# Where the residual scale is applied: to the summed products in the layer norm instead of to weight rows on GpSimd

## Chip, cores and metric

One NeuronCore of one Trainium2 chip runs the kernel. The metric is device time in microseconds, the median of several runs; a single profiled execution gives the trace.

## What is computed

The reference is a decoder trunk of two layers over 256 tokens of width 1024. Each layer has two blocks, a mixer (three kinds of attention side by side) and a channel mixer (dense SwiGLU in layer 0, top-2 of 8 experts in layer 1), and each block ends in the same way:

```python
y = hybrid_mixer(h, w_in[l], ..., w_out[l], ...)        # ends in concat(ya, yb, yc) @ w_out
x = layer_norm(DEEPNORM_ALPHA * x + (1.0 + g1) * y, ln1_g[l], ln1_b[l])
...
y = swiglu(h, w1_dense[l // 2], w3_dense[l // 2], w2_dense[l // 2])   # layer 0; ends in ... @ w2
x = layer_norm(DEEPNORM_ALPHA * x + (1.0 + g2) * y, ln2_g[l], ln2_b[l])
```

The gate (1 + g) is one row of 1024 values per layer and block, computed from the conditioning vector. Since y ends in a product with w_out or w2, the row may be multiplied into the columns of these weights or into the finished sum. The kernel holds x without the factor alpha, so its row is (1 + g) / alpha, called `grow`.

## The kernel before

All activations and weights are float32. A product is made exact enough by splitting both operands into a rounded high part and the rest, hi and lo, and adding three matmuls: hi by hi, hi by lo, lo by hi. Tokens are in two row blocks of 128 (b = 0, 1).

Weights are streamed in one fixed order (`stream`). `load_ahead` issues their loads from the SP queue into `raw` tiles of 1 MB as these come free; `split_up_to` walks the same stream, ACT writes the high half (`whi`, L374) and DVE the low half (`wlo`, L377), and a raw tile is free when both of its parts are split. The order of the instructions on each engine is that of the program (the schedule is written out by hand), so an engine that waits holds up all that stands behind it.

The stages of the span are the mixer of layer 0 (up to about 190 us), the dense block (190 to 410 us), the mixer of layer 1 (410 to 566 us) and the experts (to 1440 us). In the dense block a turn t makes 256 columns of the hidden layer (`up`, L1135 to L1137), then adds the product of the previous 256 with two row blocks of w2 (`down`, L1190) into four PSUM banks, `acc[b][hf]`, one for each row block b and column half hf. In the turns DVE also sums rows of w_ada (L527, L529) for layer 1.

`gained` (L301) multiplies raw rows of w_out and w2 by `grow` on GpSimd (POOL), two instructions of 128x1024 for each raw tile, in place, before ACT and DVE split them. Three w_out tiles of layer 0, eleven w2 tiles and four w_out tiles of layer 1 go that way, 36 instructions. The first tile of w_out in layer 0 is scaled on DVE instead (L373), between its load and its split, in two instructions of 128x1024.

`layer_norm` (L705 to L717) closes a block: for each column half it adds the PSUM bank to `xres` (L711) and takes statistics (L712), then it aggregates, POOL computes the reciprocal root (L437, L438), and DVE writes `xhat` (L717), which PE turns (L638) for the next block. The last products of a block are issued row block by row block, and within one both column halves alternate:

```python
for b in range(NB):
    for k in (3, 2, 1, 0):
        out(k, ws[k], b)
    ...
    layer_norm(acc[b], xhat, b)
    if b == 0:
        split_up_to(used[0] + 4) if l == 0 else load_ahead()
```

POOL also does the affine part of the residual (`residual`, L725 and L726, eight instructions of 128x512 for each layer norm but the last), and small sums.

## Time and profile before

| | us |
|---|---|
| median of 3 runs | 1461.44 |
| lowest, highest | 1459.02, 1462.02 |
| the profiled execution's own time | 1462.73 |
| its span in the trace | 1460.9 |

The span is what the trace covers, from the first to the last instruction; the execution's own time is 1.83 us longer, and all comparisons are made against it. A stretch of the span is named by its start and end in us from the start of the span. "Granted clock" is the share of full speed that the chip gave TensorE.

### The profile page before, as it was taken

The numbers are of one execution on the slowest core, as the hardware profiler recorded it, in microseconds if no ns is written. First come the engines' busy times: TensorE is split into PE (matmuls) and PEld (weight loads), VectorE is DVE, ScalarE is ACT, GpSimd is POOL, SyncE is SP. The second block draws the span as 40 slices with busy tenths as digits, with TensorE's granted clock in tenths as the row PEclk, the third lists the DMA queues.
The fourth block names the chain that finished last, engine by engine and source line by source line (L and its number), as shares of the span: only waits on it lengthen the run. The fifth ranks groups of instructions, "written<-read, shape, count | busy, mean of one in ns | idle before, by whom it ended". The sixth has DMA issues, their size and how long they took to land.

```text
span 1460.9 us, 20619 instructions
## 1 busy us (share of the span) xinstructions
PE 1387.4 (95%) x8017; PEld 729.5 (50%) x8017; DVE 597.4 (41%) x1063; ACT 375.7 (26%) x705; POOL 191.4 (13%) x146
## 2 busy tenths in 40 slices
PE   6999899899998899999999999999999999999994
PEld 5777689899878677223233223343233342232331
DVE  3658688999877985211120121110320110320113
ACT  2464354333345542212101112011211110211100
POOL 0202344333334420000300000000000000000000
PEclk9999899999999999999999999999999999999998
DMA  8894587688656328998999999999999999999994
GB/s 319 280 339 169 199 305 256 213 266 284 233 169 208 115 97 334 408 377 324 389 403 408 408 403 408 408 402 409 409 402 409 409 402 408 409 400 408 407 402 155
DMA packets 175497, 480.47 MB, mean 329 GB/s; under 512 B 10848, under 2 KB 44184, under 8 KB 175392
## 3 DMA queue, kind: packets, MB, share of 16 engines
q1 hardware_dynamic: 173820, 475.03, 85.7%
q10 hardware_dynamic: 1572, 4.04, 0.8%
q8 instruction: 65, 1.06, 0.3%
q14 instruction: 40, 0.33, 0.1%
HBM read 477.99 MB, written 1.05 MB: 328 GB/s over the span
## 4 chain that ended last, share of the span: by engine, by line
PE 71%; DVE 16%; issue 6%; DMA 4%; ACT 2%; POOL 1%; SPq 0%; DVEq 0%; ACTq 0%; POOLq 0%
PE bk L1570 26%; PE bk L1624 12%; PE bk L1578 7%; DVE wlo L377 7%; PE bk L1630 4%; PE bk L1085 3%; PE bk L1409 2%; PE bk L1649 2%; DVE part L529 2%; PE bk L1190 2%; DMA rawwlo<-in_w_moe 2%; PE bk L1609 1%; PE bk L561 1%; ACT whi L374 1%; DMA raw<-in_w_moe 1%
## 5 line engine op out<-in xcount | busy, mean ns | idle before, releaser
L1570 PE MATMUL bk<-raw,xe 128*64 128x512 f32 x1072 | 286.2, 597 | 3.2 <-DMA raw<-in_w_moe 3.2
L377 DVE TENSOR_TENSOR wlo<-raw,whi 128x1024 fp32r<-128x1024 f32 (+3 forms) x146 | 198.3, 1394 | 38.7 <-ACT whi L374 38.6
L1590 DVE TENSOR_TENSOR eg<-aff,bk 64x512 f32<-64x512 f32 x56 | 38.0, 679 | 387.2 <-ACT aff L1589 385.4
L1570 PEld LDWEIGHTS bk<-raw,xe 128*64 128x64 f32 x1072 | 84.0, 136 | 130.2 <-issue 118.0
L374 ACT ACTIVATE whi<-raw 128x1024 fp32r<-128x1024 f32 (+3 forms) x146 | 134.6, 975 | 15.4 <-DVE raw L373 6.0
L1624 PE MATMUL bk<-raw,egT 128*64 128x512 f32 x568 | 134.4, 600 | 0.0
L301 POOL TENSOR_TENSOR raw<-raw,grow 128x1024 f32<-128x1024 f32 x36 | 97.9, 2745 | 139.8 <-DMA raw<-in_w_dense 76.6
L1570 PE MATMUL bk<-rawwhi,xe 128*64 128x512 f32 x360 | 109.5, 601 | 2.3 <-DMA rawwhi<-in_w_moe 2.3
L1570 PE MATMUL bk<-rawwlo,xe 128*64 128x512 f32 x360 | 107.3, 592 | 0.0
L685 POOL TENSOR_TENSOR part<-vrows,cf 78x512 f32<-78x512 f32 x8 | 8.5, 1062 | 743.6 <-DVE eg L1600 714.2
L1589 ACT ACTIVATE aff<-bk 64x512 f32<-64x512 f32 x56 | 33.2, 594 | 267.1 <-PE bk L1570 267.1
L1614 DVE COPY egT<-bk 128x384 f32<-128x384 f32 (+1 forms) x24 | 11.8, 491 | 214.8 <-PE bk L1609 214.8
L1137 PE MATMUL bk<-hT,wlo 128*128 128x256 f32 x320 | 92.2, 288 | 5.1 <-DVE wlo L377 5.1
L1612 ACT ACTIVATE egT<-bk 128x384 f32<-128x384 f32 (+1 forms) x32 | 14.0, 438 | 321.6 <-PE bk L1609 321.6
L1135 PE MATMUL bk<-hT,whi 128*128 128x256 f32 x320 | 92.2, 288 | 0.9 <-ACT whi L374 0.9
L1136 PE MATMUL bk<-hT,whi 128*128 128x256 f32 x320 | 91.7, 287 | 0.0
L740 PE MATMUL bk<-whi,hT 128*128 128x384 f32 (+2 forms) x208 | 78.9, 379 | 4.8 <-ACT hT L1258 2.4
L1624 PEld LDWEIGHTS bk<-raw,egT 128*64 128x64 f32 x568 | 36.7, 136 | 78.6 <-issue 65.3
L741 PE MATMUL bk<-wlo,hT 128*128 128x384 f32 (+2 forms) x208 | 74.0, 356 | 1.9 <-DVE wlo L377 1.9
L1578 PE MATMUL bk<-raw,xe 128*32 128x512 f32 x536 | 75.0, 598 | 0.0
L742 PE MATMUL bk<-whi,hT 128*128 128x384 f32 (+2 forms) x208 | 73.8, 355 | 0.1
L1137 PEld LDWEIGHTS bk<-hT,wlo 128*128 128x128 f32 x320 | 62.5, 195 | 6.2 <-DVE wlo L377 6.2
(324 smaller groups left out, 2120.2 us busy)
## 6 DMA issues: line engine op xcount, KB each, us to landing
raw<-in_w_moe SPq DMA_DIRECT2D x205, 1024.0 KB, 14.5
rawwhi<-in_w_moe SPq DMA_DIRECT2D x131, 512.0 KB, 11.5
rawwlo<-in_w_moe SPq DMA_DIRECT2D x131, 512.0 KB, 11.4
raw<-in_w_ada SPq DMA_DIRECT2D x48, 1024.0 KB, 5.2
raw<-in_w_dense SPq DMA_DIRECT2D x33, 1024.0 KB, 9.0
raw<-in_w_in SPq DMA_DIRECT2D x16, 768.0 KB, 9.1
raw<-in_w_in SPq DMA_DIRECT2D x8, 1024.0 KB, 7.8
raw<-in_w_out SPq DMA_DIRECT2D x8, 1024.0 KB, 5.2
```

The costliest lines, as they stand in the source:

```text
L301: pool.tensor_mul(raw["sb"][:, k], raw["sb"][:, k], grow[raw["gain"]])
L374: act.activation(hi, src, AF.Copy)
L377: eng.tensor_sub(lo, src, hi.bitcast(FT))
L740: mm(pss[b][:, :w], hT[0][:, k, sl], wh[:, i % 2], start=k == 0, stop=False)
L741: mm(pss[b][:, :w], hT[0][:, k, sl], wl[:, i % 2], start=False, stop=False)
L742: mm(pss[b][:, :w], hT[1][:, k, sl], wh[:, i % 2], start=False, stop=k == KD - 1)
L1135: mm(o, w[0][:, k], hT[0][:, k], start=k == 0, stop=False)
L1136: mm(o, w[0][:, k], hT[1][:, k], start=False, stop=False)
L1137: mm(o, w[1][:, k], hT[0][:, k], start=False, stop=k == KD - 1)
L1570: mm(h[hf][q:q + 64], xe[:, k, 0:BASE], at(w, i)[:, sl], start=k == 0, stop=k == KD - 1)
L1578: mm(hov[hf][q:q + 32], xe[:, k, BASE:CAP], at(w, i)[:, sl], start=k < 2, stop=k >= KD - 2)
L1624: mm(y[64 * hf:64 * hf + 64], gT[:, j, 0:BASE], at(w, i)[:, 512 * hf:512 * hf + 512], start=c == 0 and j == 0, stop=c == 3 and j == n - 1)
```

## The change

`gained`, its calls, the flags `gain` and `late` and the DVE multiplication L373 go. `layer_norm` gets the row as `gain` and multiplies each PSUM bank by its half of the row, in place, before the addition. The last products of a block (two w_out tiles, two w2 tiles) are issued by column halves: for a row block first all products of half 0, then all of half 1. The fourth block end, behind the experts, is not touched.

```diff
--- before.py
+++ after.py
@@ -114,7 +114,6 @@
 MIX_POOL = (0, 0)
 DENSE_POOL = 0
 SUMS_AHEAD = 3
-GAIN_AHEAD = 3
 BIAS_ON_DVE = 1
 GATHER_AT = 2
 ROWS_AT = (0, 2)
@@ -150,11 +149,8 @@
 
     grow = {}
 
-    def weight(key, ap, cols=False, gain=None, late=False):
+    def weight(key, ap, cols=False):
         raw = {"ap": ap.rearrange("(k p) f -> p k f", p=128), "cols": cols}
-        if gain is not None:
-            raw["gain"] = gain
-            raw["late"] = late
         for i in (1, 0) if key[0] == "out" else (0, 1):
             unit(key, raw, i)
 
@@ -233,7 +229,7 @@
         for g in OUT_ORDER:
             if g == LAST_ADA:
                 one_ada()
-            weight(("out", l, g), a["w_out"][l][256 * g:256 * g + 256], gain=(l, 0), late=l == 0 and g > 2)
+            weight(("out", l, g), a["w_out"][l][256 * g:256 * g + 256])
         if l == 0:
             ada_weights(0, 11, 12)
             for t in range(12):
@@ -241,7 +237,7 @@
                     pair_weights([(i, (f"d{i}", t), a[f"w{i}_dense"][0][:, 256 * t:256 * t + 256])
                                   for i in (1, 3)], t > 0)
                 for d in () if t in (0, 10) else (t - 1,) if t < 11 else (9, 10):
-                    weight(("d2", d), a["w2_dense"][0][256 * d:256 * d + 256], gain=(0, 1))
+                    weight(("d2", d), a["w2_dense"][0][256 * d:256 * d + 256])
                 if t in DENSE_ADA:
                     n = DENSE_ADA[t]
                     ada_weights(1, n, n + 1)
@@ -293,12 +289,6 @@
             order_of_raws.append(raw)
         elif part == 1 and all(raw is not r for r in order_of_raws[-3:]):
             order_of_raws.append(raw)
-
-    def gained(raw):
-        if "gain" in raw and not raw["late"] and "gained" not in raw and raw["gain"] in grow:
-            raw["gained"] = True
-            for k in range(2):
-                pool.tensor_mul(raw["sb"][:, k], raw["sb"][:, k], grow[raw["gain"]])
 
     def load_ahead(most=1000):
 
@@ -346,8 +336,6 @@
         for raw in order_of_raws[loads[1]:loads[1] + SUMS_AHEAD]:
             if "ada" in raw and "sb" in raw and raw["ada"][:2] not in on_pe:
                 summed(raw)
-        for raw in order_of_raws[loads[1]:min(loads[0], loads[1] + GAIN_AHEAD)]:
-            gained(raw)
         while len(ready) <= min(n, len(stream) - 1):
             raw, part = stream[len(ready)]
             key = keys[len(ready)]
@@ -358,7 +346,6 @@
             load_ahead()
             if "sb" not in raw:
                 return
-            gained(raw)
             k, f = raw["ap"].shape[1], raw["ap"].shape[2]
             if raw["cols"]:
                 f //= 2
@@ -366,11 +353,8 @@
             else:
                 k //= 2
                 src = raw["sb"][:, k * part:k * part + k]
-            assert "gain" not in raw or raw["late"] or "gained" in raw
             hi = wsplit.tile([128, 1024], FR, name="whi", tag="whi")[:, :k * f].rearrange("p (k f) -> p k f", k=k)
             lo = wsplit.tile([128, 1024], FR, name="wlo", tag="wlo")[:, :k * f].rearrange("p (k f) -> p k f", k=k)
-            if "gain" in raw and raw["late"]:
-                vec.tensor_mul(src, src, grow[raw["gain"]][:, None, :])
             act.activation(hi, src, AF.Copy)
             many = DENSE_POOL if key[0][0] == "d" and len(key) == 3 else MIX_POOL[key[1]]
             eng = pool if many and len(ready) % many == 1 else vec
@@ -702,12 +686,14 @@
         return base.tile([128, NB, D], FT, name="xhat", tag=tag)
 
 
-    def layer_norm(y, dst, b):
+    def layer_norm(y, dst, b, gain=None):
 
         st = small.tile([128, 2, 6], FT, name="lnst")
         for h in range(2):
             sl = slice(512 * h, 512 * h + 512)
             if y is not None:
+                if gain is not None:
+                    vec.tensor_mul(y[h], y[h], gain[:, sl])
                 vec.tensor_add(xres[:, b, sl], y[h], xres[:, b, sl])
             vec.bn_stats(st[:, h], xres[:, b, sl])
         mv = small.tile([128, 2], FT, name="lnmv")
@@ -1078,10 +1064,10 @@
             tick(START_TICK[l])
             acc = [[bank() for _ in range(2)] for _ in range(NB)]
 
-            def out(k, w, b):
+            def out(k, w, b, hfs=range(2)):
                 sl = slice(128 * b, 128 * b + 128)
                 for x, wi, first in ((yT[0], 0, True), (yT[0], 1, False), (yT[1], 0, False)):
-                    for hf in range(2):
+                    for hf in hfs:
                         mm(acc[b][hf], x[:, k, sl], w[wi][:, 0, 512 * hf:512 * hf + 512],
                            start=k == 7 and first, stop=k == 0 and x is yT[1])
 
@@ -1103,11 +1089,12 @@
         split_up_to(used[0] + END_SPLIT[l])
         xhat = normal(xtag)
         for b in range(NB):
-            for k in (3, 2, 1, 0):
-                out(k, ws[k], b)
+            for hf in range(2):
+                for k in (3, 2, 1, 0):
+                    out(k, ws[k], b, (hf,))
             if b == 1 and hook is not None:
                 hook(xhat, mod)
-            layer_norm(acc[b], xhat, b)
+            layer_norm(acc[b], xhat, b, grow[l, 0])
             if b == 0:
                 split_up_to(used[0] + 4) if l == 0 else load_ahead()
         return xhat, mod
@@ -1183,10 +1170,10 @@
                     gs.append((hi, lo))
                 return gs
 
-            def part(b, t, j, g, w):
+            def part(b, t, j, g, w, hfs=range(2)):
                 sl = slice(128 * b, 128 * b + 128)
                 for gi, wi in ((0, 0), (0, 1), (1, 0)):
-                    for hf in range(2):
+                    for hf in hfs:
                         mm(acc[b][hf], g[gi][:, sl], w[wi][:, 0, 512 * hf:512 * hf + 512],
                            start=t == 0 and j == 0 and gi == 0 and wi == 0, stop=t == 10 and j == 1 and gi == 1)
 
@@ -1213,11 +1200,12 @@
             ends = [(t, j, need("d2", t, j, ahead=0)) for t in (9, 10) for j in range(2)]
             split_up_to(used[0] + END_SPLIT[2])
             for b in range(NB):
-                for t, j, w in ends:
-                    part(b, t, j, gs[t][j], w)
+                for hf in range(2):
+                    for t, j, w in ends:
+                        part(b, t, j, gs[t][j], w, (hf,))
                 if b == 1:
                     hook(xhat, mod)
-                layer_norm(acc[b], xhat, b)
+                layer_norm(acc[b], xhat, b, grow[0, 1])
                 if b == 0:
                     split_up_to(used[0] + 4)
         return xhat, mod
```

On POOL, from the rope additions of the layer 0 mixer to the end of the dense block, before (L666 rope, L301 the row scaling, L437 and L438 the reciprocal root, L650 a low half, L725 and L726 the residual):

```order
L301 TENSOR_TENSOR raw<-raw,grow 128x1024 x4
L725 TENSOR_TENSOR xres<-xhat,lnrow 128x512
L726 TENSOR_TENSOR xres<-xres,lnrow 128x512
L301 TENSOR_TENSOR raw<-raw,grow 128x1024 x2
L725 TENSOR_TENSOR xres<-xhat,lnrow 128x512
L726 TENSOR_TENSOR xres<-xres,lnrow 128x512
L301 TENSOR_TENSOR raw<-raw,grow 128x1024 x2
L725 TENSOR_TENSOR xres<-xhat,lnrow 128x512
L726 TENSOR_TENSOR xres<-xres,lnrow 128x512
```

Now, the same place (L711 and L712 are the former L725 and L726):

```order
L711 TENSOR_TENSOR xres<-xhat,lnrow 128x512
L712 TENSOR_TENSOR xres<-xres,lnrow 128x512
L711 TENSOR_TENSOR xres<-xhat,lnrow 128x512
L712 TENSOR_TENSOR xres<-xres,lnrow 128x512
L711 TENSOR_TENSOR xres<-xhat,lnrow 128x512
L712 TENSOR_TENSOR xres<-xres,lnrow 128x512
L711 TENSOR_TENSOR xres<-xhat,lnrow 128x512
L712 TENSOR_TENSOR xres<-xres,lnrow 128x512
L421 TENSOR_SCALAR lnrs<-lnmv 128x1
```

The residual's eight instructions now stand in one row, without the twenty-two scalings of w2 that stood before, between and behind them.

On DVE, in the mixer of layer 0 before the retention steps, before (L854 a low half of the attention's output, L1064 the copy of a projection):

```order
L854 TENSOR_TENSOR yT_447<-bk,yT_446 128x256
L373 TENSOR_TENSOR raw<-raw,grow 128x1024
L377 TENSOR_TENSOR wlo<-raw,whi 128x1024
L854 TENSOR_TENSOR yT_447<-bk,yT_446 128x256
L373 TENSOR_TENSOR raw<-raw,grow 128x1024
L377 TENSOR_TENSOR wlo<-raw,whi 128x1024
L1064 COPY rvg<-bk 128x512 x2
```

Now:

```order
L840 TENSOR_TENSOR yT_447<-bk,yT_446 128x256
L361 TENSOR_TENSOR wlo<-raw,whi 128x1024
L840 TENSOR_TENSOR yT_447<-bk,yT_446 128x256
L361 TENSOR_TENSOR wlo<-raw,whi 128x1024
L1050 COPY rvg<-bk 128x512 x2
```

The two scalings are gone from between the splits; the other rows stand in the same order.

On PE, the last products of the dense block, row block 0, before (bk_1902 is column half 0, bk_1903 column half 1; whi and wlo are w2, ghi and glo the hidden layer):

```order
L1190 MATMUL bk_1902<-whi_3821,ghi_3645 128x512
L1190 MATMUL bk_1903<-whi_3821,ghi_3645 128x512
L1190 MATMUL bk_1902<-wlo_3822,ghi_3645 128x512
L1190 MATMUL bk_1903<-wlo_3822,ghi_3645 128x512
L1190 MATMUL bk_1902<-whi_3821,glo_3646 128x512
L1190 MATMUL bk_1903<-whi_3821,glo_3646 128x512
```

Now (bk_1898 is half 0, bk_1899 half 1), the last three of half 0 and the first three of half 1:

```order
L1177 MATMUL bk_1898<-whi_3872,ghi_3857 128x512
L1177 MATMUL bk_1898<-wlo_3873,ghi_3857 128x512
L1177 MATMUL bk_1898<-whi_3872,glo_3858 128x512
L1177 MATMUL bk_1899<-whi_3797,ghi_3623 128x512
L1177 MATMUL bk_1899<-wlo_3798,ghi_3623 128x512
L1177 MATMUL bk_1899<-whi_3797,glo_3624 128x512
```

Twelve products of half 0 come first and twelve of half 1 behind them, where they alternated.

## Rows read from the trace of the kernel before

**Rows 1.** the page: busy time of the engines, share of the span, instructions

```profile
PE 1387.4 (95%) x8017; PEld 729.5 (50%) x8017; DVE 597.4 (41%) x1063; ACT 375.7 (26%) x705; POOL 191.4 (13%) x146
```

**Rows 2.** stretches: busy us (instructions) by engine, granted clock, DMA share, GB/s

```profile
130.00:165.00 35.00, 30.67 (x172) 23.52 (x171) 28.35 (x68) 10.92 (x19) 17.69 (x12) 0.85 0.45 163
190.00:230.00 40.00, 37.34 (x280) 33.91 (x273) 33.77 (x34) 23.51 (x39) 22.95 (x11) 1.00 0.90 317
230.00:300.00 70.00, 65.73 (x459) 61.10 (x458) 63.86 (x62) 23.08 (x35) 29.63 (x13) 0.98 0.74 250
300.00:380.00 80.00, 77.56 (x535) 72.70 (x534) 72.09 (x80) 32.70 (x45) 20.60 (x8) 0.96 0.81 280
380.00:397.00 17.00, 13.93 (x106) 12.15 (x104) 15.78 (x15) 2.97 (x5) 8.40 (x3) 0.90 0.34 113
476.00:540.00 64.00, 57.30 (x306) 45.16 (x305) 58.97 (x149) 31.36 (x70) 25.59 (x14) 0.92 0.29 100
548.00:1440.00 892.00, 882.37 (x4837) 300.71 (x4837) 159.72 (x311) 134.44 (x262) 20.09 (x20) 1.00 1.01 396
```

**Rows 3.** PE's waits, 130 to 540 us: releaser, us, times, longest

```profile
PE bk L1137 <- DVE wlo L377: 5.1, 4, 3.1
...
PE bk L1014 <- DVE rst L1003: 3.8, 2, 2.0
PE bk L1190 <- DVE wlo L377: 3.8, 1, 3.8
PE bk L850 <- ACT pT L839: 3.0, 2, 2.0
PE bk L998 <- DVE rvg L1064: 2.4, 1, 2.4
```

**Rows 4.** line L301 on POOL: duration in ns, min/median/max

```profile
L301 POOL TENSOR_TENSOR raw<-raw,grow x36: 2352/2538/3388, 134.0 to 519.4; 128x1024 f32<-128x1024 f32 x36
```

**Rows 5.** DVE's groups, 190 to 400 us: shapes, count | busy us, mean ns

```profile
L377 DVE TENSOR_TENSOR wlo<-raw,whi 128x1024 fp32r<-128x1024 f32 x63 | 105.4, 1713 | 6.1 <-ACT whi L374 6.1
L529 DVE SCALAR_TENSOR_TENSOR part<-raw,cs,part 128x512 f32<-128x512 f32 x56 | 50.1, 894 | 1.7
L1144 DVE TENSOR_TENSOR glo<-g,ghi 128x256 fp32r<-128x256 f32 x20 | 14.3, 715 | 9.7 <-ACT ghi L1143 9.7
L1140 DVE TENSOR_TENSOR g<-g,bk 128x256 f32<-128x256 f32 x20 | 8.2, 410 | 0.9 <-ACT g L1139 0.9
```

**Rows 6.** DVE in one turn of the dense loop: start us, us, instruction

```profile
330.70 4.56 DVE L377 TENSOR_TENSOR wlo<-raw,whi 128x1024 fp32r<-128x1024 f32 x2
...
339.57 3.50 DVE L377 TENSOR_TENSOR wlo<-raw,whi 128x1024 fp32r<-128x1024 f32 x3 [0.53 <-ACT whi L374]
...
349.97 1.22 DVE L377 TENSOR_TENSOR wlo<-raw,whi 128x1024 fp32r<-128x1024 f32 x1
```

**Rows 7.** POOL in the same turn

```profile
331.78 5.75 POOL L301 TENSOR_TENSOR raw<-raw,grow 128x1024 f32<-128x1024 f32 x2 [13.52 <-DMA raw<-in_w_dense]
```

**Rows 8.** DVE in the mixer of layer 1, softmax steps

```profile
482.81 1.79 DVE L805 TENSOR_SCALAR smm<-smm 128x2 f32<-128x2 f32 x1
...
490.73 0.17 DVE L805 TENSOR_SCALAR smm<-smm 128x2 f32<-128x2 f32 x1
```

**Rows 9.** DVE in the mixer of layer 0, rows of w_out scaled on DVE

```profile
141.50 1.21 DVE L373 TENSOR_TENSOR raw<-raw,grow 128x1024 f32<-128x1024 f32 x1
143.84 1.23 DVE L377 TENSOR_TENSOR wlo<-raw,whi 128x1024 fp32r<-128x1024 f32 x1 [1.12 <-ACT whi L374]
```

**Rows 10.** DVE at the end of the dense block, around the layer norm

```profile
403.45 0.69 DVE L711 TENSOR_TENSOR xres<-bk,xres 128x512 f32<-128x512 f32 x1 [0.29 <-PE bk L1190]
...
409.85 0.68 DVE L711 TENSOR_TENSOR xres<-bk,xres 128x512 f32<-128x512 f32 x1
```

**Rows 11.** line L1085 on PE: weight loads and matmuls, ns

```profile
L1085 PEld LDWEIGHTS bk<-whi,yT x128: 186/188/333, 158.0 to 561.0; 128*128 128x128 f32 x128
L1085 PE MATMUL bk<-whi,yT x128: 387/394/774, 158.1 to 561.3; 128*128 128x512 f32 x128
```

## The prediction, before the run

> **What bounds the kernel now.** I began with the page's engine totals: PE is busy 95% of the span, DVE 41%, POOL 13% [rows 1]. A share over the whole span hides that the stages differ, so the next view is the table of stretches [rows 2]. From 548 to 1440 us, the experts, PE is busy 882.37 of 892 us and the DMA engines are full (share 1.01). The change touches nothing there. That stage begins when the mixer of layer 1 ends and frees its memory, and then runs at its own pace, so a microsecond won before it moves the end by a microsecond. What counts is how much time PE loses before 548 us, and to whom.
>
> I count PE's loss in a stretch as idle time plus what a lowered clock costs, (1 - granted clock) x busy time. From [rows 2]:
> - 130 to 165 (mixer 0): 4.33 + 0.15 x 30.67 = 8.9 us
> - 190 to 230 (start of the dense block): 2.7 us
> - 230 to 300, 300 to 380, 380 to 397 (dense turns): 5.6 + 5.5 + 4.5 = 15.6 us
> - 476 to 540 (mixer 1): 6.70 + 0.08 x 57.30 = 11.3 us
>
> Together 38.5 us. PE's waits say to whom [rows 3]: in the dense block to DVE's low halves (L1137 and L1190, 8.9 us), in the mixers to DVE's rst and rvg (3.8 and 2.4 us) and to ACT's pT, which itself comes late behind DVE's softmax steps. DVE is full there: 63.86 of 70 us, 72.09 of 80, 58.97 of 64 [rows 2].
>
> Part of DVE's fullness is not work. POOL's scaling L301 takes 2.35 to 3.39 us for each of 36 instructions [rows 4]. While it runs, DVE instructions that read SBUF alone are stretched. Two low halves take 4.56 us at 330.70, where three take 3.50 at 339.57, 1.17 each [rows 6]; POOL is in L301 from 331.78 to 337.5 [rows 7]. In mixer 1 a tiny L805 takes 1.79 us beside L301 and 0.17 without [rows 8]. An instruction that reads a PSUM bank is not stretched: L1140 averages 0.41 us over the same stage [rows 5]. From 190 to 400 us the 63 low halves average 1.713 us [rows 5], so on them alone DVE loses 63 x (1.713 - 1.17) = 34 us. A few of these are due to the residual's own POOL work, which stays.
>
> **The change part by part.**
>
> *Dense block, 22 L301 removed.* The turn from 330.70 to 349.97 lasts 19.27 us [rows 6]. DVE is busy 72.09/80 of it, 17.4 us, and 2 x (2.28 - 1.17) = 2.2 us of that is the stretch of two low halves; L1144, 0.715 us on average [rows 5], gives back something over half a microsecond more. DVE then needs under 15 us and the short waits for ACT. PE needs 19.27 minus its loss, 5.5 us over 4.15 turns, or 17.9 us. So PE becomes the bound of the turn, with about 2 us to spare on DVE. Of the 15.6 us I take back 14; the rest stays as short waits. In 190 to 230 I take nothing of the 2.7 us: there the residual's eight POOL instructions move up into the place of L301, as the order on POOL shows, and stretch DVE in its stead. Bounds: 8 us (half of the loss has other causes) and 18.3 us (all of both).
>
> *Mixer 0, six L301 and two L373 removed.* Each L373 holds DVE 1.21 us, and then DVE waits 1.12 us until ACT has made the high half of the scaled rows [rows 9]. That is 4.7 us off DVE just ahead of rvg, on which PE waits 2.4 us, and of rst, on which it waits about 2 [rows 3]. The two L301 before them stretched softmax steps as well. I expect the first wait to go, half of the second, and about half of the slow clock that follows (4.6 us in the stretch): 2.4 + 1 + 2.3, say 6 us. Bounds: 0 (PE's chain of scores, rst and products is the slow part) and 8.9.
>
> *Mixer 1, eight L301 removed.* Eight stretches of about 1.6 us [rows 8] are some 13 us of DVE time, more than the 11.3 us that PE loses. The softmax chain also has round trips between PE, ACT and DVE that no scaling causes, so I take 8 us. Bounds: 4 and 11.3.
>
> *Layer norm, 12 multiplications added.* The nearest row is L711, which reads a bank and a row of SBUF: 0.69 us [rows 10]; 12 x 0.69 = 8.3 us of DVE. For row block 0 the three steps of half 0 now run beside the products of half 1, and three steps instead of four follow the last product: 0.7 us earlier. For row block 1 DVE comes late: L711 starts at 409.85, straight behind the two splits [rows 10], when its products are done, so all six steps follow, 1.4 us more and 0.7 net. PE turns that block right then. At the ends of mixer 0 and the dense block that is +0.7 us each; at the end of mixer 1 no splits stand between, and I put 0. Sum +1.4; bounds -2.1 (0.7 earlier at all three) and +8.3 (all twelve on the path).
>
> *Column halves on PE.* Two matmuls in a row used one stationary tile before, and now each follows another. The trace has a weight load of 186 to 188 ns for each matmul, 128 for 128, whether the tile is the same or not [rows 11]; nothing was shared, so I cost this at nothing. The Trainium skill says otherwise of the plan (TensorE: Matmul & The Clock Gate, Step-by-step: what each phase is for): loading is separate from multiplying so that one load can serve several matmuls. By it, the new order would give up one load of each pair.
>
> *The rest.* The order on SP and ACT is the same, and no DMA is added; a w2 tile no longer waits for POOL between landing and split. The row `grow` must now live until the layer norm, so ACT's write of the next row may wait for the last multiplication; it stands behind other ACT work, and uncovered it would cost one step, 0.7 us.
>
> Sum: -14 - 6 - 8 + 1.4 = -26.6 us. The profiled execution took 1462.73 us, which gives 1436.1; its time lies 1.29 us over the median, so against the median I predict **1435 us**.
>
> **The rivals.**
>
> *Half the gain (the next wait is close behind).* The five loads of a turn are 5.24 MB; at share 0.81 the DMA engines moved 280 GB/s [rows 2], so full engines move 346 GB/s and need 15.2 us of the 17.9 that PE needs. That fits, but the loads come in bursts as tiles come free. In the mixers the round trips may hold PE as DVE did. Half of 28 us is left, less 1.4: 1449 us. Chance 0.22.
>
> *The whole loss comes back.* 8.9 + 15.6 + 11.3 - 1.4 = 34.4 us: 1427 us. For it speaks that a low clock follows PE's own pauses. Chance 0.12.
>
> *Slower: the stretch has another cause and stays.* If DVE were slow in these places by something else, such as the DMA writes of the same stretches, PE's loss would remain and the multiplications would come on top, 1.4 to 8.3 us: 1463 to 1470, about 1465 us. It decides if a 128x1024 low half still takes over 2 us where POOL is idle. Against it stand 3.50 us for three while DMA runs, and 0.17 against 1.79 [rows 6, 8]. Chance 0.03.
>
> *The weight loads were shared.* Three block ends have 144 such matmuls; if the second of each of 72 pairs paid another 0.19 us [rows 11], that is 13.7 us: 1449 us. Chance 0.03.
>
> *It does not do what it says.* The order shows the L301 rows gone, so only the halves can fail: if DVE were let go only after both halves, every row block would have six steps behind its products, 1.4 us each at six places instead of +1.4 in all, 1442 us. I count that within the first case.
>
> **How the numbers follow.** The likeliest case, 1435 us, has 0.58, and its own range is 1428 to 1443. Half the gain has 0.22, the whole loss 0.12, shared loads 0.03, slower 0.03, and a gain too small to see 0.02. To hold 8 in 10, the range reaches over the half case and past the whole-loss case: 1424 to 1450. About 0.2%, 2.9 us, is what a measurement of this kernel can tell from no change. Faster by more: 0.94; within it 0.03; slower 0.03.
>
> **What would show it.** Right: no low half of 128x1024 over 1.3 us from 230 us on; a dense turn of 17.9 us with PE idle near zero; rvg and rst no longer waited for at length in mixer 0; the experts stage as long as before and some 27 us earlier; six DVE steps at each row block's end, three of them before its last product. Wrong: DVE instructions still stretched, turns still over 19 us, or PE waiting for loads or for ACT in DVE's place.

## The result, and the profile after

| | before | changed |
|---|---|---|
| median, us | 1461.73 | 1426.36 |
| lowest, highest | 1459.02, 1467.72 | 1425.36, 1427.23 |
| ratio, 95% interval | | 0.9759 [0.9732, 0.9786] |

The kernel is 35.4 us faster by the medians; the forecast was 26.4 us, 1435 us with a range of 1424 to 1450. In the two profiled executions the span goes from 1460.9 to 1424.4 us. The measured time lies outside the likeliest case's own range of 1428 to 1443 and inside the stated one. The page's first line answers to [rows 1]:

```profile
PE 1375.5 (97%) x8017; PEld 719.7 (51%) x8017; DVE 546.0 (38%) x1073; ACT 376.5 (26%) x705; POOL 91.2 (6%) x110
```

POOL lost 100 us of work and DVE 51 us, although DVE has ten instructions more. Where PE's loss went is seen in the stretches, which answer to [rows 2]. Two of them are cut by the same instructions in both kernels: the dense turns, from their first product (L1135, now L1122) to the first of the last products, and mixer 1 from its first product for attention scores (L825, now L811) to a late one with the probabilities (L850, now L836). Before:

```profile
206.29:397.83 191.54, 179.74 (x1263) 167.27 (x1261) 174.28 (x170) 69.54 (x99) 77.65 (x30) 0.96 0.75 257
477.65:540.43 62.78, 56.08 (x297) 43.74 (x296) 58.92 (x150) 30.18 (x68) 24.47 (x14) 0.92 0.29 100
```

Now, with mixer 0 ahead of them and the experts behind:

```profile
130.00:165.00 35.00, 34.92 (x218) 26.21 (x217) 26.64 (x78) 16.93 (x29) 4.97 (x6) 1.00 0.50 180
199.97:371.63 171.66, 171.66 (x1262) 161.60 (x1261) 135.68 (x173) 72.16 (x102) 13.28 (x8) 1.00 0.84 287
453.42:503.79 50.37, 50.07 (x298) 39.08 (x297) 44.63 (x145) 29.87 (x68) 5.95 (x6) 1.00 0.37 125
511.50:1403.50 892.00, 882.22 (x4836) 300.56 (x4836) 162.37 (x315) 134.31 (x262) 20.07 (x20) 1.00 1.01 396
```

In the dense turns PE is busy without a gap at a granted clock of 1.00, for the same products in 19.9 us less. In the mixers' stretches 0.08 and 0.30 us of idle time are left, where there were 4.33 and 6.70. The experts' stretch, as long as that of before, has the same busy time to 0.15 us: it was moved, not changed. PE's waits from 130 to 503 us answer to [rows 3]:

```profile
PE bk L767 <- DVE ltn L780: 4.2, 2, 4.0
PE bk L727 <- DVE wlo L361: 1.4, 1, 1.4
PE bk L858 <- DVE wlo L361: 1.0, 1, 1.0
PE bk L1148 <- DVE hT L614: 0.6, 1, 0.6
PE bk L622 <- DVE xhat L703: 0.6, 1, 0.6
...
```

The waits for low halves in the dense loop, for rst, rvg and pT are gone. What is left lies at the joints: the latent norm at the start of mixer 1 (L767, 4.5 us before) and the ends and starts of blocks. DVE's groups from 190 to 400 us answer to [rows 5]: the same 63 low halves take 1.290 us where they took 1.713, the sums of w_ada 0.751 for 0.894, L1131 (L1144 before) 0.492 for 0.715. The instruction that reads a PSUM bank, L1127 (L1140), takes what it took.

```profile
L361 DVE TENSOR_TENSOR wlo<-raw,whi 128x1024 fp32r<-128x1024 f32 x63 | 78.6, 1290 | 5.8 <-ACT whi L358 5.8
L513 DVE SCALAR_TENSOR_TENSOR part<-raw,cs,part 128x512 f32<-128x512 f32 x56 | 42.1, 751 | 1.7
L1131 DVE TENSOR_TENSOR glo<-g,ghi 128x256 fp32r<-128x256 f32 x20 | 9.8, 492 | 9.7 <-ACT ghi L1130 9.7
L1127 DVE TENSOR_TENSOR g<-g,bk 128x256 f32<-128x256 f32 x20 | 8.4, 418 | 16.0 <-ACT g L1126 16.0
```

In mixer 1 the tiny step of [rows 8] (L791 now) took 0.733 us on average and takes 0.206, over twelve of them in the stretches above, before and now:

```profile
L805 DVE TENSOR_SCALAR smm<-smm 128x2 f32<-128x2 f32 x12 | 8.8, 733 | 0.4
```

```profile
L791 DVE TENSOR_SCALAR smm<-smm 128x2 f32<-128x2 f32 x12 | 2.5, 206 | 0.4
```

One turn, as in [rows 6], now runs on DVE from glo at 314.77 to glo at 332.43, 17.66 us where it was 19.27, and the pair of low halves at its end takes 2.36 us, not 4.56. The turns before were uneven, 17.1 to 22.3 us from glo to glo; now six in a row take 17.4 to 17.7.

```profile
314.77 0.42 DVE L1131 TENSOR_TENSOR glo<-g,ghi 128x256 fp32r<-128x256 f32 x1 [0.48 <-ACT ghi L1130]
...
329.25 2.36 DVE L361 TENSOR_TENSOR wlo<-raw,whi 128x1024 fp32r<-128x1024 f32 x2
...
332.43 0.43 DVE L1131 TENSOR_TENSOR glo<-g,ghi 128x256 fp32r<-128x256 f32 x1 [0.49 <-ACT ghi L1130]
```

The end of the dense block on DVE, against [rows 10] (L696 the multiplication, L697 the addition, L698 the statistics):

```profile
374.69 0.70 DVE L696 TENSOR_TENSOR bk<-bk,grow 128x512 f32<-128x512 f32 x1
375.50 0.69 DVE L697 TENSOR_TENSOR xres<-bk,xres 128x512 f32<-128x512 f32 x1
376.22 0.69 DVE L698 BATCH_NORM_STATS2 lnst<-xres 128x6 f32<-128x512 f32 x1
377.41 0.70 DVE L696 TENSOR_TENSOR bk<-bk,grow 128x512 f32<-128x512 f32 x1 [0.50 <-PE bk L1177]
...
381.56 1.82 DVE L361 TENSOR_TENSOR wlo<-raw,whi 128x768 fp32r<-128x768 f32 x2
383.30 0.69 DVE L696 TENSOR_TENSOR bk<-bk,grow 128x512 f32<-128x512 f32 x1
...
388.68 0.81 DVE L703 TENSOR_SCALAR xhat<-xres,lnmv,lnrs 128x1024 f32<-128x1024 f32 x1 [0.95 <-POOL lnrs L422]
```

For row block 0 the three steps of half 0 are done before half 1's last product, for which DVE waits 0.50 us. For row block 1 all six follow the two splits in one piece, and xhat is 0.6 us late for PE (the wait for L703 above).

The row of xhat for row block 1 ends a block, and its start divides the span alike in every kernel. Each mixer is divided once more, where PE starts its first product for the attention scores (us; the blocks by rows on DVE, the last column is the span less what stands before it). This table serves all experiments:

| kernel | to the scores of mixer 0 | rest of mixer 0 | dense block | to the scores of mixer 1 | rest of mixer 1 | experts to end |
|---|---|---|---|---|---|---|
| before | 96.6 | 96.83 | 220.65 | 63.61 | 87.74 | 895.5 |
| changed | 98.1 | 89.00 | 201.61 | 64.74 | 75.52 | 895.5 |
| halves_only | 98.1 | 96.81 | 221.30 | 63.62 | 85.24 | 896.6 |
| no_halves | 97.8 | 90.59 | 203.52 | 63.72 | 77.36 | 897.4 |
| pool_beside | 97.8 | 89.01 | 222.88 | 63.62 | 75.53 | 897.5 |
| pool_memset3 | 97.7 | 89.03 | 201.58 | 63.70 | 75.53 | 898.9 |
| w2_moved | 96.3 | 96.40 | 201.60 | 63.69 | 88.79 | 896.4 |
| wout_moved | 96.6 | 89.04 | 221.04 | 63.75 | 75.55 | 900.0 |
| no_gain | 96.6 | 87.83 | 200.76 | 63.66 | 74.23 | 897.3 |
| after_again | 97.7 | 89.00 | 201.63 | 63.62 | 75.53 | 896.8 |
| residual_dve | 98.0 | 89.00 | 201.53 | 62.82 | 75.54 | 899.6 |
| splits_pool | 96.3 | 89.52 | 202.40 | 63.70 | 75.52 | 898.7 |

The change took 7.8 us from mixer 0, 19.0 from the dense block and 12.2 from mixer 1, 39.1 us together. The span shows 36.5 of them: in its profiled execution the changed kernel was 1.5 us longer up to the first scores and 1.1 us longer at the start of mixer 1. Both come and go where nothing was changed (halves_only, after_again). The experts' stage varies by 4.5 us in the same way, so a single span says little below that. The rest of mixer 0, the dense block and the rest of mixer 1 repeat to 0.1 us among kernels that have the change there; in kernels that have a stage as before it varies by up to 1.1 us.

### The profile page after: what moved, and what is told of

Same layout as the page of the kernel before. It is cut to its first block, busy times and chain, and to the rows that moved or that the text cites. A ratio compares the mean times of both kernels' runs of the same rounds, so it can differ in the third digit from the quotient of the medians.

```text
span 1424.4 us, 20550 instructions
## 1 busy us (share of the span) xinstructions
PE 1375.5 (97%) x8017; PEld 719.7 (51%) x8017; DVE 546.0 (38%) x1073; ACT 376.5 (26%) x705; POOL 91.2 (6%) x110
## 4 chain that ended last, share of the span: by engine, by line
PE 84%; DVE 5%; issue 5%; DMA 3%; ACT 2%; POOL 1%; SPq 0%; DVEq 0%; ACTq 0%; POOLq 0%
PE bk L1558 27%; PE bk L1612 13%; PE bk L1566 7%; PE bk L1618 4%; PE bk L1177 4%; PE bk L1122 3%; PE bk L1123 3%; PE bk L1124 3%; PE bk L1071 2%; PE bk L1397 2%; PE bk L1637 2%; PE bk L726 2%; PE bk L728 2%; PE bk L727 2%; DMA rawwlo<-in_w_moe 2%
## 5 line engine op out<-in xcount | busy, mean ns | idle before, releaser
L361 DVE TENSOR_TENSOR wlo<-raw,whi 128x1024 fp32r<-128x1024 f32 (+3 forms) x146 | 170.2, 1201 | 35.6 <-ACT whi L358 35.3
L1122 PE MATMUL bk<-hT,whi 128*128 128x256 f32 x320 | 90.3, 282 | 0.0
L1123 PE MATMUL bk<-hT,whi 128*128 128x256 f32 x320 | 90.2, 282 | 0.0
L726 PE MATMUL bk<-whi,hT 128*128 128x384 f32 (+2 forms) x208 | 78.5, 378 | 1.6 <-ACT hT L1246 0.9
L1558 PEld LDWEIGHTS bk<-rawwlo,xe 128*64 128x64 f32 x360 | 32.1, 137 | 62.7 <-issue 59.0
L1122 PEld LDWEIGHTS bk<-hT,whi 128*128 128x128 f32 x320 | 60.2, 188 | 0.1
```

Source lines behind the costliest of these rows:

```text
L361: eng.tensor_sub(lo, src, hi.bitcast(FT))
L726: mm(pss[b][:, :w], hT[0][:, k, sl], wh[:, i % 2], start=k == 0, stop=False)
L1122: mm(o, w[0][:, k], hT[0][:, k], start=k == 0, stop=False)
L1123: mm(o, w[0][:, k], hT[1][:, k], start=False, stop=False)
L1558: mm(h[hf][q:q + 64], xe[:, k, 0:BASE], at(w, i)[:, sl], start=k == 0, stop=k == KD - 1)
```

## The experiments

Theory 1: POOL reading SBUF holds up DVE's instructions that have their operands there, PE waits for DVE, and its granted clock is lower where it waits (0.96 in the dense turns before, 1.00 now). Theory 2: the splits waited for POOL, so the chain from landing to product was too long. Theory 3: the order of the last products carried the gain. The kernels ran in three groups, each on one chip beside the kernel before: halves_only, no_halves, pool_beside and pool_memset (before: 1460.65 us), then w2_moved, wout_moved, no_gain and pool_memset3 (1465.77), then the last four (1461.89). Ratios are to the kernel before of the same group.

**halves_only**: before, with the loops over hf outside those over the tiles.

```diff
-            for k in (3, 2, 1, 0):
-                out(k, ws[k], b)
+            for hf in range(2):
+                for k in (3, 2, 1, 0):
+                    out(k, ws[k], b, (hf,))
```

> The kernel before with the column-half order of the last products alone; the rows of w_out and w2 are still scaled on POOL and DVE. Theory 1 (POOL's reading holds up DVE, PE waits for DVE): no change, 1461 us within 3. Theory 2 (a split waits for POOL's scaling, the chain from landing to product is too long): the same, 1461. Theory 3 (the order of the last products is worth the time): near the changed kernel, below 1440. The rival of the prediction, shared weight loads: 72 pairs that pay another 0.19 us, some 1475.

Measured 1464.05 us, ratio 1.0021 [0.9998, 1.0045]: no gain, so theory 3 falls. The weight loads are settled by the changed kernel itself: it has 8017 of them for 8017 matmuls, as before [rows 1]. The 48 last products of the dense block, first and last row before and in the changed kernel:

```profile
397.83 0.71 PE L1190 MATMUL bk<-whi,ghi 128*128 128x512 f32 x2
...
408.46 0.62 PE L1190 MATMUL bk<-whi,glo 128*128 128x512 f32 x2
```

```profile
371.63 0.49 PE L1177 MATMUL bk<-whi,ghi 128*128 128x512 f32 x1
...
382.43 0.39 PE L1177 MATMUL bk<-whi,glo 128*128 128x512 f32 x1
```

From first start to last end that is 11.25 us alternating and 11.19 by halves. By the Trainium skill (TensorE: Matmul & The Clock Gate, Step-by-step: what each phase is for), where one load can serve several matmuls, the new order would have lost a load for each pair; in this trace it costs the same either way.

**no_halves**: the changed kernel with that order undone.

```diff
-            for hf in range(2):
-                for k in (3, 2, 1, 0):
-                    out(k, ws[k], b, (hf,))
+            for k in (3, 2, 1, 0):
+                out(k, ws[k], b)
```

> The changed kernel with the column halves alternating again, the scale still in the layer norm. Theory 1: the three steps of half 0 no longer run beside products, so row block 0 of each of three block ends comes 3 x 0.7 = 2.1 us later on DVE, and PE, which had 0.2 to 0.6 us of waiting there, waits for most of it: 1428 to 1433. Theory 3 (the order carries the gain): back to 1455 or more.

Measured 1432.52 us, ratio 0.9815 [0.9789, 0.984]: some 6 us more than the changed kernel. Mixer 0, the dense block and mixer 1 lose 1.6, 1.9 and 1.8 us by the table, 5.3 together, and PE's waits for xhat rise from 0.8 to 5.8 us:

```profile
PE bk L622 <- DVE xhat L703: 5.8, 6, 1.5
```

So the order is worth nothing alone and 5 to 6 us once the multiplication is there: it pays for what the layer norm got to do.

**pool_beside**: the changed kernel with POOL's 22 multiplications back in the dense block; nothing waits for them.

```diff
+    def beside(raw):
+        if "d2" in raw and dead and (0, 1) in grow and "beside" not in raw:
+            raw["beside"] = True
+            for k in range(2):
+                pool.tensor_mul(dead[0][:, k], raw["sb"][:, k], grow[0, 1])
```

> The changed kernel, with 22 POOL multiplications of 128x1024 put back at their places in the dense block, of the same raw rows by the same row, but written to a tile that nothing reads; no split and no product waits for them. Theory 1: DVE's low halves take over 2 us beside them again, the dense turn goes from 17.64 back to some 19.3 us, and the dense block's part of the gain, 18 to 20 us, is lost: 1440 to 1447. Theory 2 (the wait of the splits for POOL was the loss): 1426, with DVE stretched or not. Theory 3: 1426.

Measured 1447.78 us, ratio 0.9917 [0.9892, 0.9943], a little over the range expected: 21.6 us more than pool_memset, below, in the same group, and the table puts the loss into the dense block alone (222.88 us for 201.61). Theory 2 falls: no split waited for POOL. PE waits for low halves once more, its two longest waits from 187 to 400 us:

```profile
PE bk L1140 <- DVE wlo L375: 4.9, 3, 3.7
PE bk L1193 <- DVE wlo L375: 4.2, 3, 3.6
```

It waits for no load, and in the dense block the queue that issues the loads waits for DVE, PE and one transfer, never for POOL; so the loss is not that POOL held the raw tiles longer. The rows show how the two engines take turns, DVE and then POOL in one turn:

```profile
306.38 4.54 DVE L375 TENSOR_TENSOR wlo<-raw,whi 128x1024 fp32r<-128x1024 f32 x2
307.52 3.41 DVE L375 TENSOR_TENSOR wlo<-raw,whi 128x1024 fp32r<-128x1024 f32 x1
310.85 0.41 DVE L1143 TENSOR_TENSOR g<-g,bk 128x256 f32<-128x256 f32 x1
311.74 1.73 DVE L1147 TENSOR_TENSOR glo<-g,ghi 128x256 fp32r<-128x256 f32 x1 [0.48 <-ACT ghi L1146]
```

```profile
307.46 5.72 POOL L302 TENSOR_TENSOR aux<-raw,grow 128x1024 f32<-128x1024 f32 x2 [13.53 <-DMA raw<-in_w_dense]
309.80 3.38 POOL L302 TENSOR_TENSOR aux<-raw,grow 128x1024 f32<-128x1024 f32 x1
```

POOL starts at 307.46, 0.06 us before DVE's second low half. That one ends at 310.93, 1.13 us after the end of POOL's first instruction; the low half ahead of it, undisturbed, took 1.14 us (306.38 to 307.52). So it stood still until 309.80. POOL's second instruction then lasts 3.38 us, 1.13 of them until DVE is done, and ends at 313.18. The tiny glo, issued at 311.74, ends at 313.47, 0.29 us later, while L1143, which reads a bank, took 0.41 us in between. A turn costs DVE 2.3 us on the low half and 1.3 on glo. This is what the Trainium skill states (SBUF — State Buffer, SBUF: two separate sides, and Who interferes with whom): whichever starts first, a DVE instruction with two SBUF inputs or a POOL instruction that reads SBUF, has the shared ports for its whole instruction, and a DVE instruction with at most one SBUF input, outside its two-port modes, is not concerned. The rows of the low halves agree to a few hundredths of a us. One input in SBUF does not by itself keep an instruction clear: L805 of [rows 8] has one, and took 1.79 us for 0.17; whether it ran in a two-port mode no row shows.

**pool_memset** and **pool_memset3**: the same places, but POOL reads one column and then only writes, once or three times.

```diff
-                pool.tensor_mul(dead[0][:, k], raw["sb"][:, k], grow[0, 1])
+                pool.tensor_mul(dead[0][:, k, 0:1], raw["sb"][:, k, 0:1], grow[0, 1][:, 0:1])
+                for _ in range(3):
+                    pool.memset(dead[0][:, k], 0.0)
```

> As the kernel with the 22 unread multiplications, but POOL reads one column of the raw tile and the row (so that it starts when it did) and then only writes 1024 columns. Theory 1 in the form that reading is what holds up DVE: the low halves stay at 1.2 us and the time at 1426 to 1429. Theory 1 in the form that any POOL instruction on SBUF holds up DVE: stretched in proportion to the time of the writing instructions, 1430 to 1445. The Trainium skill (SBUF — State Buffer, Who interferes with whom) says that a DVE instruction with two SBUF inputs contends with a GpSimd instruction that reads SBUF and not with one that only writes it; by it, 1426.

> As the kernel in which POOL only writes, but each writing of 1024 columns three times: 66 x 0.955 us = 63 us of POOL time in the dense block, as much as the 22 unread multiplications took (63.5 us). Theory 1, reading is what holds up DVE: 1426 to 1429, low halves at 1.2 us. Theory 1 in the other form, POOL's time on SBUF counts whatever it does: 1440 to 1447.

Measured 1426.14 us, ratio 0.9772 [0.9745, 0.9799], and 1426.12 us, 0.9733 [0.971, 0.9755], in two groups. With three writings POOL is as long in SBUF as with the multiplications (63.0 against 63.5 us), and neither the time nor the low halves show it. POOL's group in pool_beside, then in pool_memset3:

```profile
L302 POOL TENSOR_TENSOR aux<-raw,grow 128x1024 f32<-128x1024 f32 x22 | 63.5, 2911 | 115.2 <-DMA raw<-in_w_dense 115.2
```

```profile
L304 POOL MEMSET aux<- 128x1024 f32 x66 | 63.0, 955 | 3.8
```

DVE's low halves in pool_memset3, 190 to 400 us:

```profile
L377 DVE TENSOR_TENSOR wlo<-raw,whi 128x1024 fp32r<-128x1024 f32 x63 | 80.1, 1312 | 6.8 <-ACT whi L374 6.8
```

In pool_beside they average 1.643 us. It is POOL's reading, not its being busy, that holds DVE up, as the Trainium skill says in the section that the expectation names. The kind of operation does not explain it: in splits_pool, below, a subtraction on POOL holds DVE up as well.

**w2_moved** and **wout_moved**: before, with the change made in the dense block alone, and in the two mixers alone.

```diff
-                    weight(("d2", d), a["w2_dense"][0][256 * d:256 * d + 256], gain=(0, 1))
+                    weight(("d2", d), a["w2_dense"][0][256 * d:256 * d + 256])
...
-                layer_norm(acc[b], xhat, b)
+                layer_norm(acc[b], xhat, b, grow[0, 1])
```

> The kernel before with only the dense block changed: w2 unscaled, the scale in its layer norm, its last products by column halves; w_out is scaled as before (six L301 and two L373 in the mixer of layer 0, eight L301 in that of layer 1). Theory 1: the dense block gains what the trace of the changed kernel shows for it, 19 to 20 us, and the mixers nothing: 1441 to 1443 us. The prediction's own terms would give 1448 (14 less 0.7). A rival, that the gains of the stages are not additive because a block that ends earlier only meets a later wait: 1448 or more, and then the other kernel below would keep less than the rest.

> The other part alone: w_out unscaled in both mixers, the scale in their two layer norms, their last products by column halves; w2 is scaled on POOL as before. Theory 1: 6 to 7 us in the mixer of layer 0 and 10 to 11 in that of layer 1: 1443 to 1446. The prediction's terms: 6 + 8 - 0.7, 1448. If the parts add, the gains of this kernel and of the other together are those of the whole change, some 35 us.

Measured 1445.17 us, ratio 0.9871 [0.9848, 0.9894], and 1445.53 us, 0.9864 [0.984, 0.9887]. The first is above the 1441 to 1443 expected, with a kernel before that is 4 us slower in this group. The medians are 20.6 and 20.2 us below that of before, together 40.8; pool_memset3, in effect the changed kernel, is 39.7 below it. The parts add, and by the table each left the other's stages as they were, within 1.1 us. No later wait took anything back.

**no_gain**: the changed kernel without its twelve multiplications, so that three block ends lack the factor.

```diff
-                if gain is not None:
-                    vec.tensor_mul(y[h], y[h], gain[:, sl])
```

> The changed kernel without the twelve multiplications of the layer norm: the factor (1 + g)/alpha is left out of three block ends. DVE has 12 x 0.7 = 8.4 us less to do. The prediction's term: 1.4 us on the path, 1424 to 1425.5. If the column halves hide all of it: 1426. If all twelve are on the path: 1418.

Measured 1422.92 us, ratio 0.9722 [0.9701, 0.9744], 3.2 us under pool_memset3 of the same group; the intervals of the two ratios overlap, so the medians give the price to a us or two only. By the table mixer 0, the dense block and mixer 1 are 1.2, 0.8 and 1.3 us shorter than in pool_memset3, 3.3 together.

**after_again, residual_dve, splits_pool, both**: can the rest be had? residual_dve moves the residual's 24 instructions from POOL to DVE; splits_pool lets POOL make the two low halves between the row blocks, ahead of the first layer norm; both does the two.

```diff
-                    pool.tensor_mul(xres[:, b, sl], xhat[:, b, sl], rows[:, 0, sl])
-                    pool.tensor_add(xres[:, b, sl], xres[:, b, sl], rows[:, 1, sl])
+                    vec.tensor_mul(xres[:, b, sl], xhat[:, b, sl], rows[:, 0, sl])
+                    vec.tensor_add(xres[:, b, sl], xres[:, b, sl], rows[:, 1, sl])
...
+            if b == 0 and l == 0:
+                split_on_pool(used[0] + 4)
             layer_norm(acc[b], xhat, b, grow[l, 0])
```

> The changed kernel itself, so that the three kernels below have it on the same chip: 1426 us within 2.

> The changed kernel with the affine part of the residual on DVE (8 instructions of 128x512 at some 0.69 us for each of three layer norms) and not on POOL. In the changed kernel they hold up DVE's low halves by 6.2 us at 200 to 222 and by 7.7 us at 404 to 425 (durations above the shortest of their shape). Theory 1: DVE gets back 6.2 and 7.7 for 2 x 5.5 us, so it ends level or a little ahead, and the wait of 1.4 us for a low half at 405 goes: 1423 to 1426. If POOL's reading did not matter, 11 us of DVE work would be added where DVE is nearly full: 1430 or more.

> The changed kernel with the two low halves that DVE makes between the layer norms of the row blocks (2.35 us at the end of mixer 0, 1.82 at the end of the dense block) made on POOL, and issued ahead of the first layer norm, beside DVE's steps that read a PSUM bank. Theory 1: those steps have one operand in SBUF and are not held up, xhat of row block 1 comes 1.7 to 2.3 us earlier, PE's waits of 0.5 to 1.0 us there go and with them part of the lower clock at 392 to 395: 1422 to 1425. If POOL's reading holds up any DVE instruction, or POOL is late with the halves: 1427 to 1430.

> Both of these changes together: the sum of the two, 1420 to 1425 by theory 1.

Measured 1425.62 us, 0.9751 [0.9738, 0.9765]; 1426.26, 0.9752 [0.9737, 0.9767]; 1429.63, 0.9774 [0.9759, 0.9788]; 1425.64, 0.9748 [0.9735, 0.9762]. None beats the changed kernel. residual_dve comes out level: its 24 instructions, 0.68 to 0.69 us each, are 16.5 us of work, but DVE's busy time rises by 2.9 us only (545.8 to 548.7), because holding up went away. The thirteen low halves of 128x1024 from 190 to 222 us take 1.220 us on average where they took 1.557 in after_again. The table shows 0.8 us won at the start of mixer 1, too little for the medians, and the wait of 1.4 us for a low half near 404 is still there.

splits_pool was expected to win and does not; both misses its 1420 to 1425 too. The median of splits_pool is 4.0 us over that of after_again, of which the table shows 0.5 in mixer 0 and 0.8 in the dense block; the rest is not located. At the end of mixer 0 POOL and then DVE:

```profile
173.29 2.41 POOL L368 TENSOR_TENSOR wlo<-raw,whi 128x1024 fp32r<-128x1024 f32 x1 [18.97 <-ACT whi L365]
176.31 2.40 POOL L368 TENSOR_TENSOR wlo<-raw,whi 128x1024 fp32r<-128x1024 f32 x1 [0.61 <-ACT whi L365]
178.79 0.19 POOL L428 TENSOR_SCALAR lnrs<-lnmv 128x1 f32<-128x1 f32 x1
```

```profile
174.30 0.69 DVE L704 TENSOR_TENSOR xres<-bk,xres 128x512 f32<-128x512 f32 x1
...
179.65 0.81 DVE L710 TENSOR_SCALAR xhat<-xres,lnmv,lnrs 128x1024 f32<-128x1024 f32 x1 [3.69 <-POOL lnrs L429]
```

The steps that read a bank were left alone beside POOL, as expected: L704 takes its 0.69 us. But POOL itself was late, the second case of the expectation: the reciprocal root stands behind its second low half, DVE waits 3.69 us for it instead of 0.95, and PE 1.48 us for xhat. At the end of the dense block, DVE and then POOL:

```profile
372.38 2.26 DVE L570 TENSOR_TENSOR part<-part,bg 1x512 f32<-1x512 f32 x1
374.57 1.80 DVE L601 SCALAR_TENSOR_TENSOR acol<-modc,cols 128x8 f32<-128x8 f32 x1
...
382.10 0.81 DVE L710 TENSOR_SCALAR xhat<-xres,lnmv,lnrs 128x1024 f32<-128x1024 f32 x1 [0.95 <-POOL lnrs L429]
```

```profile
372.24 4.12 POOL L368 TENSOR_TENSOR wlo<-raw,whi 128x768 fp32r<-128x768 f32 x2 [155.18 <-ACT whi L365]
```

Here POOL was done before the bank-reading steps began, and met two small instructions with SBUF operands instead: 2.26 us for what takes 0.67, and 1.80 for 0.15. PE waits 1.41 us for the xhat at 382.10. The 0.6 us that PE waited there for row block 1 are gone, and the longer wait for row block 0 is new at both ends.

## Why the prediction was right, and where its sum was short

- **Mechanism: right.** "PE loses to DVE, and DVE's fullness is partly not work": shown for the dense block by pool_beside (put back, with nothing waiting for it, POOL's work costs 21 us) and pool_memset3 (the same POOL time without reading costs nothing). The turn became PE-bound at 17.66 us (17.9 said); no 128x1024 low half from 231 to 368 us is over 1.23 us. In the mixers wout_moved shows that the change there brings the gain, and the rows that the holding up went with it; what POOL's scaling and what the two scalings on DVE did to it was not taken apart.
- **Dense block, -14 of bounds 8 to 18.3: the step that failed most.** The turns are 19.9 us shorter, outside the bounds; the end of the block, from its last products on, is 0.8 us longer (0.7 said). PE's loss had been read as 15.6 + 2.7 = 18.3 us. Of this 1.6 were left as short waits and 2.7 put at nothing, and both came back, with 1.6 more. That the reading is a little short shows in the very stretch of the turns: idle time plus (1 - granted clock) x busy time is 11.80 + 0.04 x 179.74 = 19.0 us there. A matmul's row is 0.28 us long where the next starts 0.12 us later (L1123 and its neighbours), so a gap counted from a row's modelled end is too short; that this is the reason is not shown, and the clock is read to 0.01 only.
- **The 2.7 us at 190 to 230, put at nothing** because the residual would hold DVE up in the place of L301. It does so, but by less. Before, four L301 ran in one piece, then four low halves beside them on DVE; behind these stood ghi, for which PE waited 2.0 us. Now the residual's first instruction starts only at 203.85, when the row it reads has landed, and the same four low halves take half the time (POOL and DVE before; DVE now):

```profile
204.40 11.43 POOL L301 TENSOR_TENSOR raw<-raw,grow 128x1024 f32<-128x1024 f32 x4 [11.04 <-ACT grow L597]
206.90 12.23 DVE L377 TENSOR_TENSOR wlo<-raw,whi 128x1024 fp32r<-128x1024 f32 x4
```

```profile
200.57 5.72 DVE L361 TENSOR_TENSOR wlo<-raw,whi 128x1024 fp32r<-128x1024 f32 x4
```

- **Mixer 0, -6 of bounds 0 to 8.9, and mixer 1, -8 of bounds 4 to 11.3: too little.** Without the multiplications (no_gain against before, by the table) they are 9.0 and 13.5 us shorter, both beyond the bounds, the first barely. In mixer 0 half of the wait for rst and half of the slow clock had been held back, in mixer 1 a part for round trips between PE, ACT and DVE. No such part shows: the waits for rst, rvg and pT went, and of those for p 0.2 us are left; ACT had only been late behind DVE.
- **Layer norm, +1.4: too little.** no_gain gives 3.2 us by the medians and 3.3 by the stages, inside the bounds of -2.1 to 8.3. The end of mixer 1, put at 0 because no splits stand there, has 1.3 of it: the six steps of row block 1 follow those of row block 0 without a pause all the same. Counted up to where PE turns xhat instead, the three ends have 0.2, 1.7 and 0.4 us, so the price is 2 to 3 us.
- **Column halves 0: right, and for the reason given.** 11.19 against 11.25 us for 48 products; the rival of shared loads (1449) falls. That DVE would be let go after half 0 is seen in the rows of L696 above; otherwise 5 to 6 us were lost (no_halves), near the 7 of that case (1442).
- **The rivals.** What happened is the second, the whole loss comes back: 1427 us said with a chance of 0.12, 1426.36 measured. That it is met to 1 us is in part luck. It had 35.8 us coming back and 1.4 to pay; by the stages 42.4 came back and 3.3 were paid, and the profiled execution lost 2.6 us where nothing was changed. "Half the gain" had more chance and nothing spoke for it in the end: DMA share in the turns is 0.84 and PE waits for no load there. The slower case, a stretch of other origin, falls with pool_beside and pool_memset3. The chances of the faster cases add up to 0.95, not 0.94; nothing hangs on it.

## What to carry to other kernels

Before giving an idle engine elementwise work, look at what the busy engine beside it reads: here 98 us of "free" POOL time and the two scalings on DVE cost some 40 us of span, and the same multiplication on the sums, in PSUM, costs 2 to 3. When a wait that dominates a stretch is traced to one cause, ask of each allowance held back for other causes which row shows them at work; here none did, and the rival that took all of PE's loss back was the right one. Cut stages by the same instructions in every kernel: so cut, the changed stages repeat to 0.1 us, while a whole span moves by several us in places that nobody touched.

## What was not expected of the hardware

- The holding up is all or nothing and goes by instruction: 0.15 us of DVE work became 1.80, and a 128x256 low half 1.73 for 0.43, by the rest of the POOL instruction that happened to be running. For their length, short DVE instructions lose most.
- POOL is held up as well: its 128x1024 multiplication takes 2.38 us at the least in pool_beside and 3.38 beside a low half, and a multiplication of one column took 1.29 us in pool_memset3 where the next took 0.19:

```profile
312.37 1.29 POOL L302 TENSOR_TENSOR aux<-raw,grow 128x1 f32<-128x1 f32 x1 [11.26 <-DMA raw<-in_w_dense]
...
316.65 0.19 POOL L302 TENSOR_TENSOR aux<-raw,grow 128x1 f32<-128x1 f32 x1
```
- POOL's writing of 128x1024 elements takes 0.955 us; it does not hold DVE up, nor is it held up (0.952 to 0.975 us in all of pool_memset).
